# A hybrid decoder layer on one core: the first stage with c as one row, sums of squares as columns, h modulated twice on ScalarE, whole modulation rows, and a block's products by kind

## The chip, the core and the metric

The kernel runs on one core of a Trainium2 chip. The metric is the device time of one execution in microseconds (us). Before the change it is 1109.52 us, the median of three runs (1110.96, 1109.22, 1109.52). Less is better.

## What is computed

One layer of a decoder on 512 tokens of width 1024, everything in float32: a modulated RMSNorm, a mixer of three branches (a state-space scan, dilated window attention, multi-scale pooling), and an MLP with squared ReLU. The change touches only the beginning: the conditioning vector, the first norm, and the first two of the products of h with the columns of w_in, called Q and K.

```python
cond = silu(c)                                    # c is 1 x 1024
sh1, sc1, g1, sh2, sc2, g2 = split(cond @ w_ada + b_ada, 6)
h = rms(x, norm1_w) * (1 + sc1) + sh1             # 512 x 1024
z, xbc, dt_raw, q, k, v, u, gates = split(h @ w_in)
x = x + g1 * mixer(q, k, v, u, gates, z, xbc, dt_raw)
h = rms(x, norm2_w) * (1 + sc2) + sh2
x = x + g2 * (square(relu(h @ w_ff1)) @ w_ff2)
```

## The kernel before

**Layout.** Activations lie with features on partitions: x is held as eight tiles xT[k] of 128 features by 512 tokens. A *block* k, in what follows, is one such step of 128 features. The result h is kept as eight such tiles too, each as a rounded part (hh) and the remainder (hl), and as copies of both with the tokens sorted by residue modulo four (rh, rl). The bulk of the work is steps of 12 products on TensorE (PE): for 128 features and 512 output columns, four accumulators, and for each three products of 512 columns (low x high, high x high, high x low of the split operands; mm3 in the code). Weights are split the same way: ScalarE (ACT) casts the raw weight to a rounded part (wh), and VectorE (DVE) subtracts it for the rest (wl).

**Buffers.** 59 blocks of 128x512 are handed out and taken back by name (blk, free), eight PSUM banks likewise. Later weights come as pairs of blocks, 128x1024, through three pools of three buffers each: raw, wh and wl (wstream, wsplit; lines 272 and 273). One weight pair feeds two steps, 24 products.

**The first stage** (from line 334) is written as one schedule by hand for VectorE, ScalarE, TensorE and SyncE (SP): there each engine does its work in the order of the code. c comes by two transfers of SP, each of 512 values spread over all 128 partitions (crow), and goes through Silu. Then SP brings the eight tiles of x, with vec (per-feature vectors: biases, norm weights) and the identity matrix (cst) in between, and for each block two rows of w_ada as four half rows (wa, 128x512 each, line 231) and two raw weights of Q and K (wst). The sums of squares for the norm: ScalarE squares the eight tiles, VectorE adds them in pairs, and TensorE multiplies them with ones over 512 columns, so that the sums stand on all partitions; four VectorE instructions with the identity (diag, line 416) take them back to columns, ScalarE takes the root, VectorE improves the reciprocal by a Newton step. The four columns are turned into a row again by diagonal matrices and four products with ones (rp). Warm-up products fill TensorE's waits (WARM, line 394).

A block then runs so: four dots of half a w_ada row with crow on VectorE (line 368) and three instructions on one column (lines 374 to 377) give the scale and the shift of the 128 features (A1); ScalarE scales xT (u, line 450), VectorE multiplies with the norm's row R1 (line 451), ScalarE adds the shift and rounds (hh, line 454), VectorE takes the remainder (hl, line 459), ScalarE makes the two copies by residue (line 445). ScalarE and VectorE split the block's two raw weights (lines 383 and 387). TensorE does the block's 24 products, 12 of Q and 12 of K, accumulator by accumulator.

**Behind the first stage** the order of each engine is no longer that of the code: a list scheduler places each instruction at build time where its priority and the buffers it needs allow it. Lines that are marked with high_priority (the weight stream, the copies out of PSUM) are taken earlier. What follows the stage: ScalarE copies q and k out of PSUM (line 324), makes 32 sums of squares of them, one for each 128 columns (sqj, line 511), and TensorE goes on with the next product of 512 columns, whose weights come through the raw, wh and wl pools. I call it Q+1 (accumulators psacc_848 to 851 before, psacc_790 to 793 after). Between two of its weight pairs stand 16 small products for the step sizes of the scan (psdt, lines 737 to 740), which use a small weight wd that ScalarE casts and VectorE subtracts (lines 731, 732).

**Columns of w_ada for later** (parts 2 to 5) are taken in the background, by half rows with crow (ada_later); crow's two blocks are given back at the end of that.

## Time and profile before

| quantity | value |
|---|---|
| median of three runs | 1109.52 us |
| the profiled execution's own time | 1109.32 us |
| its span in the trace | 1107.5 us |
| TensorE busy (PE) / weight loads (PEld) | 99% / 83% of the span |
| VectorE (DVE) / ScalarE (ACT) / GpSimd (POOL) busy | 54% / 46% / 0% |
| TensorE's granted clock | 1.00 |
| moved by DMA | 134.45 MB, mean 121 GB/s |

The profile shows one execution. Engines that are off the end's path may be idle at no cost. A row such as "L368 DVE SCALAR_TENSOR_TENSOR wa<-wa,crow 128x512 ..." is line 368 of the kernel, the engine, the operation, and out <- in by the program's names. In rows of the timeline the first number is the start, the second the time that the row's instructions cover, both in us, and the brackets hold the idle time before them and what ended it. In rows of groups the numbers behind the bar are the total in us and the mean of one in ns. In rows of waits they are the total in us, the number of waits and the longest.

### The profile page before, as it was taken

To read this page: it belongs to the slowest core of one execution; us is meant where nothing else is said; L and a number is where in the kernel's file an instruction comes from. 1 tells how busy PE (TensorE), PEld (TensorE's weight loads), DVE (VectorE), ACT (ScalarE), POOL (GpSimd) and SP (SyncE) were. 2 spreads that over 40 slices of the span, in tenths; PEclk is the share of its full clock that TensorE was granted. 3 is DMA by queue.
4 is the path that set the end of the run, shared out by engine and by line. 5 is a ranking of instruction groups with operands and counts; after the bars stand their busy time and mean duration, and the time that the engine had idled before them with its cause. 6 is when DMAs were issued, how large, how long until landed. Compare 5 with 4: busy or idle time off the path is not lost.

```text
span 1107.5 us, 14079 instructions
## 1 busy us (share of the span) xinstructions
PE 1098.5 (99%) x5414; PEld 916.5 (83%) x5414; DVE 597.1 (54%) x1210; ACT 507.5 (46%) x953; POOL 0.2 (0%) x4
## 2 busy tenths in 40 slices
PE   8999999999999999999999999999999999999998
PEld 6878888888887888888888888899888888888887
DVE  6964773574766778478832433665544223455241
ACT  6895885643596456425422223343433122344120
POOL 0000000000000000000000000000000000000000
PEclk9999999999999999999999999999999999999999
DMA  9943343444543453322323432440133222222241
GB/s 337 314 141 106 115 157 100 133 134 130 186 130 96 125 163 121 119 83 77 123 96 124 143 95 96 142 163 2 60 105 100 96 95 95 96 96 95 95 133 38
DMA packets 49348, 134.45 MB, mean 121 GB/s; under 512 B 5617, under 2 KB 6385, under 8 KB 49281
## 3 DMA queue, kind: packets, MB, share of 16 engines
q1 hardware_dynamic: 47696, 130.81, 36.4%
q10 hardware_dynamic: 1584, 2.75, 0.8%
q8 instruction: 42, 0.69, 0.3%
q14 instruction: 26, 0.20, 0.1%
HBM read 131.41 MB, written 2.13 MB: 121 GB/s over the span
## 4 chain that ended last, share of the span: by engine, by line
PE 89%; ACT 4%; DMA 4%; DVE 2%; issue 1%; SPq 0%; ACTq 0%; DVEq 0%
PE psacc L287 27%; PE psacc L289 27%; PE psacc L288 27%; DMA wa<-in_w_ada_dram 1%; PE psS L566 1%; DMA M<-prow 1%; ACT wh L272 1%; PE psy L880 1%; PE pso L682 1%; PE psyo L888 1%; PE pso L680 1%; DVE conv L798 1%; DMA wst<-in_w_in_dram 0%; PE pskT L550 0%; PE pspT L663 0%
## 5 line engine op out<-in xcount | busy, mean ns | idle before, releaser
L273 DVE TENSOR_TENSOR wl<-raw,wh 128x1024 fp32r<-128x1024 f32 x161 | 196.9, 1223 | 335.5 <-ACT wh L272 333.9
L272 ACT CAST wh<-raw 128x1024 fp32r<-128x1024 f32 x161 | 168.9, 1050 | 365.5 <-PE psacc L288 321.4
L287 PE MATMUL psacc<-hl,wh 128*128 128x512 f32 x416 | 166.4, 400 | 0.6 <-ACT prev L843 0.5
L289 PE MATMUL psacc<-hh,wl 128*128 128x512 f32 x416 | 162.3, 390 | 0.0
L288 PE MATMUL psacc<-hh,wh 128*128 128x512 f32 x416 | 162.1, 390 | 0.0
L287 PEld LDWEIGHTS psacc<-hl,wh 128*128 128x128 f32 x416 | 78.2, 188 | 18.3 <-issue 1.2
L288 PE MATMUL psacc<-ah,wh 128*128 128x512 f32 (+1 forms) x242 | 92.1, 381 | 0.0
L288 PEld LDWEIGHTS psacc<-hh,wh 128*128 128x128 f32 x416 | 78.2, 188 | 16.8 <-issue 1.4
L287 PE MATMUL psacc<-al,wh 128*128 128x512 f32 (+1 forms) x242 | 92.1, 381 | 0.0
L289 PE MATMUL psacc<-ah,wl 128*128 128x512 f32 (+1 forms) x242 | 92.0, 380 | 0.0
L289 PEld LDWEIGHTS psacc<-hh,wl 128*128 128x128 f32 x416 | 78.1, 188 | 16.6
L288 PE MATMUL psacc<-gh,wh 128*128 128x512 f32 x224 | 87.2, 389 | 0.0
L287 PE MATMUL psacc<-gl,wh 128*128 128x512 f32 x224 | 87.2, 389 | 0.0
L289 PE MATMUL psacc<-gh,wl 128*128 128x512 f32 x224 | 87.0, 389 | 0.0
L287 PE MATMUL psacc<-wl,rh 128*128 128x512 f32 x192 | 77.1, 402 | 0.0
L289 PE MATMUL psacc<-wh,rl 128*128 128x512 f32 x192 | 75.2, 392 | 0.0
L288 PE MATMUL psacc<-wh,rh 128*128 128x512 f32 x192 | 74.9, 390 | 0.0
L237 DVE SCALAR_TENSOR_TENSOR wa<-wa,crow 128x512 f32<-128x512 f32 x64 | 43.3, 688 | 19.3 <-DMA wa<-in_w_ada_dram 19.0
L287 PEld LDWEIGHTS psacc<-al,wh 128*128 128x128 f32 x242 | 45.5, 188 | 8.9
L288 PEld LDWEIGHTS psacc<-ah,wh 128*128 128x128 f32 x242 | 45.5, 188 | 8.7
L289 PEld LDWEIGHTS psacc<-ah,wl 128*128 128x128 f32 x242 | 45.5, 188 | 8.7
L287 PEld LDWEIGHTS psacc<-gl,wh 128*128 128x128 f32 x224 | 42.1, 188 | 8.7
(350 smaller groups left out, 1955.8 us busy)
## 6 DMA issues: line engine op xcount, KB each, us to landing
raw<-in_w_in_dram SPq DMA_DIRECT2D x80, 512.0 KB, 3.5
raw<-in_w_ff_dram SPq DMA_DIRECT2D x64, 512.0 KB, 3.5
wa<-in_w_ada_dram SPq DMA_DIRECT2D x96, 256.0 KB, 4.1
wst<-in_w_in_dram SPq DMA_DIRECT2D x16, 256.0 KB, 5.4
M<-prow SPq DMA_DIRECT2D x16, 256.0 KB, 3.3
raw<-in_w_ssd_out_dram SPq DMA_DIRECT2D x8, 512.0 KB, 3.5
raw<-in_w_pool_out_dram SPq DMA_DIRECT2D x8, 512.0 KB, 3.4
raw<-in_w_out_dram SPq DMA_DIRECT2D x8, 512.0 KB, 3.5
```

Of the source, the lines that this page charges most:

```text
L237: V.scalar_tensor_tensor(wa[i], wa[i], 1.0, crow[i], ALU.mult, ALU.mult, accum_out=d[:, i : i + 1])
L272: S.copy(wh, raw)
L273: V.tensor_tensor(wl, raw, wh.bitcast(F32), ALU.subtract)
L287: mm(ps, lhsT=wh, rhs=xl, start=first, stop=False)
L288: mm(ps, lhsT=wh, rhs=xh, start=False, stop=False)
L289: mm(ps, lhsT=wl, rhs=xh, start=False, stop=last)
L566: mm(so[b], lhsT=qT[:, b * P : (b + 1) * P], rhs=kT[:, (b + 1) * P - n : (b + 1) * P], start=True, stop=True)
L680: mm(od, lhsT=vs[kb][:, hs], rhs=pT[b // 2][:, cs : cs + P], start=(b == 0), stop=False, skip_group_check=True)
L682: mm(ov[:, b, :], lhsT=vs[b][:, hs], rhs=pT[0][:, b * P : (b + 1) * P], start=False, stop=(gi == 2 and b == 3), skip_group_check=True)
L798: V.scalar_tensor_tensor(t[:, i:], x[:, : T - i], cw[:, 3 - i, n : n + 1], t[:, i:], ALU.mult, ALU.add)
L880: mm(yp[half * 64 : half * 64 + 64, cs], lhsT=X[c][:, (2 * j + half) * 64 : (2 * j + half + 1) * 64], rhs=Ms[half][:, cs], start=True, sto ...
L888: mm(op[:, cs], lhsT=prev[c][:, j * P : (j + 1) * P], rhs=CT[:, cs], start=True, stop=True)
```

## The change

It rewrites the first stage and leaves the rest of the code as it is.

- **c** is loaded as one row of 1024 on one partition, in two transfers that ScalarE's queue issues, goes through Silu there, and is spread over the partitions by two products with a row of ones into PSUM; VectorE copies it to crow2, which is a small tile of its own and no longer two of the 59 blocks. The filler tile gap shrinks from 464 to 448 columns.
- **vec and the identity** are loaded by GpSimd's queue (POOL) and no longer by SP's.
- **Sums of squares**: VectorE adds the first four tiles' squares, and then three of the other four; TensorE takes the sums as columns, by products of each 128 tokens with one column of ones (square_sums). No diagonal is needed to get columns; ScalarE reads the four sums from PSUM twice, for the root and for the variance. The root's table load comes after the squares. Three of the four diagonals for the row R are made on ScalarE.
- **Modulation rows** come whole, 128x1024 (ada_whole), into buffers of the pools raw, wh and wl in turn, those that the weight stream uses later. A block's two dots are over whole rows (line 379 of the changed kernel), the norm's weight goes into the dot, and one addition of a table pre (line 511) gives scale and shift together.
- **h**: VectorE multiplies xT with R1 (normed, line 475), one instruction on ScalarE scales, shifts and rounds to hh, and a second one makes the same in float32 in place (u, line 478); VectorE subtracts (line 482).
- **Products** of a block by kind: high x high and high x low of Q, the same of K, then low x high of both; in the last block Q's are done before K's.
- **Warm-up** products: 12, 1, 5, 5 and 6 in place of 18, 12 and 6.

What the built programs of the two kernels have on ScalarE behind the first stage, before: rl is the last copy by residue, wh a weight pair's cast, wd the small weight, q and k the copies out of PSUM, sqj the square sums, rkr the root for k.

```order
L445 CAST rh_68_265<-hh_249 128x512
L445 CAST rl_76_273<-hl_257 128x512
L272 CAST wh_854<-raw_852 128x1024
L731 CAST wd_887<-wdt_885 128x8x16
L272 CAST wh_892<-raw_890 128x1024
L324 COPY q_739<-psacc_282 128x512
...
L324 COPY k_793<-psacc_289 128x512
...
L511 ACTIVATE sqj_829,ssk_798<-k_793 128x128
L272 CAST wh_950<-raw_948 128x1024
L188 ACTIVATE rkr_832<-ssk_798,epsc_89 128x16
```

And after the change:

```order
L470 CAST rl_74_269<-hl_253 128x512
L271 CAST wh_796<-raw_794 128x1024
L323 COPY q_681<-psacc_282 128x512
...
L323 COPY k_735<-psacc_289 128x512
...
L546 ACTIVATE sqj_771,ssk_740<-k_735 128x128
L766 CAST wd_829<-wdt_827 128x8x16
L189 ACTIVATE rkr_774<-ssk_740,epsc_88 128x16
L271 CAST wh_834<-raw_832 128x1024
L271 CAST wh_892<-raw_890 128x1024
```

Two weight casts and wd's stood ahead of the copies before; now one cast stands there, and wd's cast and the second pair's follow the last square sum.

TensorE at the same place, before: psacc are Q+1's accumulators with weights wh and wl, psdt the small products.

```order
L289 MATMUL psacc_851<-wh_854,rl_70_267 128x512
L287 MATMUL psacc_848<-wl_893,rh_63_260 128x512
...
L289 MATMUL psacc_851<-wh_892,rl_72_269 128x512
L738 MATMUL psdt_920<-hh_242,wd_887 32x512
L740 MATMUL psdt_920<-hl_250,wd_887 16x512
...
L738 MATMUL psdt_920<-hh_249,wd_887 32x512
L287 MATMUL psacc_848<-wl_951,rh_65_262 128x512
```

And after the change:

```order
L288 MATMUL psacc_793<-wh_796,rl_68_263 128x512
L773 MATMUL psdt_862<-hh_238,wd_829 32x512
L775 MATMUL psdt_862<-hl_246,wd_829 16x512
...
L772 MATMUL psdt_862<-hl_251,wd_829 16x512
L286 MATMUL psacc_790<-wl_835,rh_61_256 128x512
...
L288 MATMUL psacc_793<-wh_834,rl_70_265 128x512
L773 MATMUL psdt_862<-hh_243,wd_829 32x512
...
L773 MATMUL psdt_862<-hh_245,wd_829 32x512
L286 MATMUL psacc_790<-wl_893,rh_63_258 128x512
```

The small products stood behind two weight pairs (48 products) in one run of 16; now eleven of them stand behind the first pair (24 products), and five behind the second pair.

VectorE in one turn of the stage's loop (k = 1, which makes ready block 2), before: wa are half rows of w_ada, A the scale and shift, wsl the low parts of Q's and K's raw weights, hl the remainder of h.

```order
L368 SCALAR_TENSOR_TENSOR wa_349,dot_361<-wa_349,crow_78 128x512
L459 SCALAR_TENSOR_TENSOR hl_251<-u_98_319,A_26_127,hh_243 128x512
L368 SCALAR_TENSOR_TENSOR wa_350,dot_361<-wa_350,crow_79 128x512
L368 SCALAR_TENSOR_TENSOR wa_353,dot_372<-wa_353,crow_78 128x512
L374 SCALAR_TENSOR_TENSOR A_27_128<-dot_361,bsc_33_134 128x1
L375 TENSOR_TENSOR A_27_128<-A_27_128,vec_76 128x1
L368 SCALAR_TENSOR_TENSOR wa_354,dot_372<-wa_354,crow_79 128x512
L387 TENSOR_TENSOR wsl_366<-wst_357,wsh_365 128x512
L377 SCALAR_TENSOR_TENSOR A_27_128<-dot_372,vec_76 128x1
L451 TENSOR_TENSOR u_111_379<-u_111_379,R_60_239 128x512
L387 TENSOR_TENSOR wsl_369<-wst_359,wsh_368 128x512
```

And after the change, with wada the whole rows:

```order
L389 TENSOR_TENSOR wsl_309<-wst_300,wsh_308 128x512
L389 TENSOR_TENSOR wsl_312<-wst_302,wsh_311 128x512
L482 TENSOR_TENSOR hl_247<-u_86_294,hh_239 128x512
L475 TENSOR_TENSOR u_96_345<-xT_6_81,R_58_236 128x512
L379 SCALAR_TENSOR_TENSOR wada_347,dot_355<-wada_347,vec_76,crow_78 128x1024
L379 SCALAR_TENSOR_TENSOR wada_349,dot_355<-wada_349,crow_78 128x1024
L511 TENSOR_TENSOR A_26_124<-dot_355,pre_130 128x2
```

Eleven instructions became seven; the low part of h and the norm's product now stand ahead of the dots.

The diff, cut to its core:

```diff
-WARM = (18, 12, 6)
+WARM = (12, 1, 5, 5, 6)
...
-    small([P, 464], "gap")
-    crow = [blk("crow") for _ in range(2)]
+    small([P, 448], "gap")
+    crow2 = small([P, 2, T], "crow")
+    crow = [crow2[:, i, :] for i in range(2)]
...
-            if not background:
-                free(*crow)
...
+        c1 = [blk("c1") for _ in range(2)]
         for i in range(2):
-            nc.sync.dma_start(crow[i], a["c"][:, i * T : (i + 1) * T].broadcast_to([P, T]))
+            nc.scalar.dma_start(c1[i][:1], a["c"][:, i * T : (i + 1) * T])
+        nc.gpsimd.dma_start(vec, a["vec"])
+        nc.gpsimd.dma_start(cst[:, :P], a["const"][:, :P])
...
+        homes = [(raws, "raw"), (wsp, "wh"), (wsp, "wl")]
+
+        def ada_whole(part, k):
+            pool, tag = homes[0]
+            homes.append(homes.pop(0))
+            w = pool.tile([P, 2, T], F32, tag=tag, name=uid("wada"))
+            src = a["w_ada"][part * 8 + k].rearrange("p (i t) -> p i t", i=2)
+            if k:
+                nc.sync.dma_start(w, src)
+            else:
+                for i in range(2):
+                    nc.sync.dma_start(w[:, i, :], src[:, i, :])
+            return w
+
         for k in range(8):
             nc.sync.dma_start(xT[k], a["x"][k])
-            if k == 0:
-                nc.sync.dma_start(vec, a["vec"])
-            if k == 1:
-                nc.sync.dma_start(cst[:, :P], a["const"][:, :P])
-        wa = [ada_load(1, 0)]
-        wa.append(ada_load(0, 0))
+        wa = [ada_whole(1, 0), ada_whole(0, 0)]
...
-        for i in range(2):
-            S.activation(crow[i], crow[i], AF.Silu)
-        S.activation(junk1, epsc, AF.Sqrt)
...
-            x = wa[i][half]
-            V.scalar_tensor_tensor(x, x, 1.0, crow[half], ALU.mult, ALU.mult, accum_out=dots[k, i][:, half : half + 1])
-            free(x)
-        def dot_end(k, i):
-            d, o = dots[k, i], A1[k][:, i : i + 1]
-            if i == 0:
-                V.scalar_tensor_tensor(o, d[:, 0:1], bsc1[:, k : k + 1], d[:, 1:2], ALU.add, ALU.add)
-                V.tensor_tensor(o, o, vc("norm1_w", k), ALU.mult)
-            else:
-                V.scalar_tensor_tensor(o, d[:, 0:1], vc("b_ada", k), d[:, 1:2], ALU.add, ALU.add)
+        pre = small([P, 8, 2], "pre")
+
+        def dot_half(k, i, half, d):
+            x = wa[i][:, half, :]
+            V.scalar_tensor_tensor(x, x, vc("norm1_w", k) if i == 0 else 1.0, crow[half], ALU.mult, ALU.mult, accum_out=d)
+
+        def dot(k, i, d):
+            V.scalar_tensor_tensor(wa[i], wa[i], vc("norm1_w", k) if i == 0 else 1.0, crow2, ALU.mult, ALU.mult, accum_out=d)
...
+        def square_sums(s, first=False, last=False):
+            for b in range(4):
+                mm(sp[:, b : b + 1], lhsT=s[:, b * P : (b + 1) * P], rhs=ones[:, 0:1], start=first and b == 0, stop=last and b == 3, skip_group_check=True)
...
+        cps = [psm("c") for _ in range(2)]
+        for i in range(2):
+            S.activation(c1[i][:1], c1[i][:1], AF.Silu)
+            mm(cps[i], lhsT=ones[:1], rhs=c1[i][:1], start=True, stop=True)
+        for k in range(8):
+            square(k)
+        S.activation(junk1, epsc, AF.Sqrt)
+        warm(WARM[1])
+        add(0, 1)
+        add(1, 2)
+        add(2, 3)
+        V.tensor_copy(crow[0], cps[0])
+        square_sums(sq[3], first=True)
+        warm(WARM[2])
+        add(4, 5)
+        add(5, 6)
+        square_sums(sq[6])
+        square_sums(sq[7], last=True)
+        V.tensor_copy(crow[1], cps[1])
+        free(sq[3], sq[6], sq[7], *cps, *c1)
+        V.scalar_tensor_tensor(pre[:, :, 0], vc("b_ada", 8, 8), 1.0, vc("norm1_w", 0, 8), ALU.add, ALU.mult)
+        V.tensor_copy(pre[:, :, 1], vc("b_ada", 0, 8))
...
+        S.activation(rt, sp[:, :4], AF.Sqrt, scale=1.0 / D, bias=epsc)
+        S.activation(var, sp[:, :4], AF.Identity, scale=1.0 / D, bias=epsc)
...
-            V.tensor_scalar(dg[b], ident, r[:, b : b + 1], None, ALU.mult)
+            if b == 0:
+                V.tensor_scalar(dg[b], ident, r[:, b : b + 1], None, ALU.mult)
+            else:
+                S.mul(dg[b], ident, r[:, b : b + 1])
...
-        def high(k, R):
-            u = us[k] = blk("u1")
-            if k:
-                S.mul(u, xT[k], A1[k][:, 0:1])
-                V.tensor_tensor(u, u, R, ALU.mult)
-            else:
-                V.scalar_tensor_tensor(u, xT[k], A1[k][:, 0:1], R, ALU.mult, ALU.mult)
-            S.activation(hh[k], u, AF.Identity, bias=A1[k][:, 1:2])
-            return by_residue(0, k)
+        def normed(k, R, ts=slice(0, T)):
+            if k not in us:
+                us[k] = blk("u1")
+            V.tensor_tensor(us[k][:, ts], xT[k][:, ts], R[:, ts], ALU.mult)
+
+        def modulate(k, o, ts=slice(0, T)):
+            S.activation(o[:, ts], us[k][:, ts], AF.Identity, bias=A1[k][:, 1:2], scale=A1[k][:, 0:1])
 
         def low(k):
             u = us.pop(k)
-            i = V.scalar_tensor_tensor(hl[k], u, A1[k][:, 1:2], hh[k].bitcast(F32), ALU.add, ALU.subtract)
+            i = V.tensor_tensor(hl[k], u, hh[k].bitcast(F32), ALU.subtract)
...
+            modulate(k, us[k])
+            w_low(Q, k)
+            w_low(K, k)
+            edgeV = low(k)
             if k < 7:
-                wa = [ada_load(1, k + 1), ada_load(0, k + 1)]
+                normed(k + 1, R1)
+                wa = [ada_whole(1, k + 1), ada_whole(0, k + 1)]
                 w_load(k + 1)
-                dot(k + 1, 0, 0)
-                if k:
-                    low(k)
-                dot(k + 1, 0, 1)
+                d = small([P, 2], "dot", 4)
+                dot(k + 1, 0, d[:, 0:1])
+                dot(k + 1, 1, d[:, 1:2])
+                V.tensor_tensor(A1[k + 1], d, pre[:, k + 1, :], ALU.add)
                 w_high(Q, k + 1)
                 w_high(K, k + 1)
-                by_residue(1, k)
-                dot(k + 1, 1, 0)
-                dot_end(k + 1, 0)
-                dot(k + 1, 1, 1)
-                w_low(Q, k + 1)
-                dot_end(k + 1, 1)
-                high(k + 1, R1)
-                w_low(K, k + 1)
-                if k == 6:
-                    edgeV = low(7)
-                    edgeS = by_residue(1, 7)
+            by_residue(0, k)
+            edgeS = by_residue(1, k)
+            if k < 7:
+                modulate(k + 1, hh[k + 1])
             th, tl = toks(hh[k], False), toks(hl[k], False)
-            for ch, ps in ((Q, qps), (K, kps)):
-                wh, wl = wparts[ch, k]
+            def products(ch, ps, t, w, first=False, last=False):
                 for j in range(4):
-                    mm3(ps[j], th[:, j, :], tl[:, j, :], wh, wl, k == 0, k == 7)
+                    mm(ps[j], lhsT=t[:, j, :], rhs=w, start=first, stop=last)
+
+            two = (Q, qps, *wparts[Q, k]), (K, kps, *wparts[K, k])
+            for ch, ps, wh, wl in two:
+                products(ch, ps, th, wh, first=k == 0)
+                products(ch, ps, th, wl)
+                if k == 7:
+                    products(ch, ps, tl, wh, last=True)
+            for ch, ps, wh, wl in two:
+                if k < 7:
+                    products(ch, ps, tl, wh)
                 free(wh, wl)
     nc.sync.dma_start(cst[:, P:ncut], a["const"][:, P:ncut])
     free(R1)
```

68 lines of the change are left out of this document (28 added, 40 removed).

## The prediction

> **What bounds the kernel now.** I read the page first, then the list of TensorE's waits, then the timeline stage by stage, then the groups of instructions for durations. Line 1 of the page:
> ```profile
> PE 1098.5 (99%) x5414; PEld 916.5 (83%) x5414; DVE 597.1 (54%) x1210; ACT 507.5 (46%) x953; POOL 0.2 (0%) x4
> ```
> TensorE is the bound almost throughout. What it waited for (total, times, longest):
> ```profile
> PE pssx L406 <- DVE sq L405: 2.6, 1, 2.6
> PE psacc L287 <- ACT hh L454: 0.5, 2, 0.4
> PE psacc L287 <- ACT prev L843: 0.5, 1, 0.5
> ```
> Behind the first stage about 1 us of waiting is left in a millisecond. So a change to the first stage moves the end one for one, and so does any wait that it opens later. The stretches (us, then busy time and count of PE, PEld, DVE, ACT, POOL, clock, DMA share, GB/s): the head, the first two blocks, blocks two to eight, two weight pairs of the next product (Q+1), and the dt products:
> ```profile
> 0.00:20.26 20.26, 16.09 (x90) 12.51 (x90) 9.61 (x38) 10.73 (x20) 0.20 (x4) 1.00 0.92 324
> 20.26:27.64 7.38, 6.77 (x27) 4.65 (x27) 7.35 (x20) 6.13 (x9) 0.00 (x0) 1.00 1.04 374
> 65.43:76.31 10.88, 10.88 (x49) 8.93 (x48) 3.76 (x19) 10.88 (x69) 0.00 (x0) 1.00 0.21 69
> 76.31:79.80 3.49, 3.49 (x17) 1.51 (x16) 2.57 (x5) 3.47 (x7) 0.00 (x0) 1.00 0.39 88
> ```
> The third row holds 48 products: 10.88 / 48 = 0.227 us each, so a block's 24 take 5.44. The last row holds 15 of the 16 dt products: 0.233 each. Real products start at 20.26; call the end of the stage E, here 65.43.
>
> **The head: what the change takes away.**
> ```profile
> 0.73 0.86 SPq L336 DMA_DIRECT2D crow<-in_c_dram  x2
> 4.51 0.63 ACT L358 ACTIVATE crow<-crow 128x512 f32<-128x512 f32 x1 [2.29 <-DMA crow<-in_c_dram]
> 10.00:12.00 2.00, 1.99 (x5) 0.58 (x4) 1.32 (x2) 1.95 (x4) 0.00 (x0) 1.00 1.05 386
> 11.58 0.63 ACT L401 ACTIVATE sq<-xT 128x512 f32<-128x512 f32 x1
> 15.57 0.30 ACT L418 ACTIVATE rxr<-rxs,epsc 128x4 f32<-128x4 f32 x1 [3.36 <-DVE diag L416]
> 16.26 0.17 DVE L423 RECIPROCAL rxy<-rxr 128x4 f32<-128x4 f32 x1
> 17.06 0.88 DVE L430 TENSOR_SCALAR diag<-cst,rxy 128x128 f32<-128x128 f32 x4
> 20.26 0.50 PE L287 MATMUL psacc<-wsl,hh 128*128 128x512 f32 x1 [0.37 <-ACT hh L454]
> ```
> The queue is saturated (share 1.05 at 386 GB/s, 0.68 us for 256 KB). Two such transfers of c go: the last square starts, its row of x just landed, at 11.58; less 2 x 0.68 that is 10.2. Bound below: a first landing near 4.5 (an estimate, by vec's 4.4 in a row further down) and seven more rows at 0.68 is 9.3, with vec and cst in the queue 9.6. I take 10.2.
>
> The last square ends at 10.8. Sums as columns: two groups of four blocks, two passes each, still follow the last addition. The price of a short pass is that of the warm-up matmuls, 0.11 ((2.84 - 0.28) / 23):
> ```profile
> 14.40 2.84 PE L394 MATMUL pswarm<-ones 128*128 128x128 f32 x24
> 6.24 1.28 ACT L359 ACT_TABLE_LOAD   x1
> ```
> 16 x 0.11 = 1.8, with its tail 12.8. The square root's table load now stands behind the squares: 10.7 + 1.28 + 0.2 = 12.2, hidden by 0.6; if the sums were ready sooner it would be the next thing late. Root 0.30, then reciprocal and three small instructions (0.8 from 16.26 to 17.06 in the trace), and a semaphore: r at 14.0, against 17.06 before.
>
> From r to the first product the old chain takes 3.2 us. The new one: diagonals and their products 1.05, half a normed block 0.40 (half of L453's 0.74, below), one half-row dot 0.61, two dependent small additions 0.4, half a modulation 0.5, and semaphores, some 0.4: 3.35. First product at 17.35.
>
> Durations for the block loop, from the groups up to 55 us, with a pair of 1024-wide instructions from the timeline:
> ```profile
> L368 DVE SCALAR_TENSOR_TENSOR wa<-wa,crow 128x512 f32<-128x512 f32 x30 | 20.1, 688 | 0.6 <-DMA wa<-in_w_ada_dram 0.6
> L454 ACT ACTIVATE hh<-u,A 128x512 fp32r<-128x512 f32 x7 | 5.1, 724 | 7.8 <-DVE u L451 5.3 <-DVE u L453 2.6
> L453 DVE SCALAR_TENSOR_TENSOR u<-xT,A,psrx 128x512 f32<-128x512 f32 x1 | 0.7, 742 | 0.0
> L383 ACT CAST wsh<-wst 128x512 fp32r<-128x512 f32 x16 | 9.1, 620 | 0.0
> 78.71 2.29 DVE L273 TENSOR_TENSOR wl<-raw,wh 128x1024 fp32r<-128x1024 f32 x2
> ```
> Back to back, a 512-wide VectorE instruction takes 0.61 and a 1024-wide one 1.07 to 1.22; whole-row dots are not in the trace, and I take 1.14. From the first half modulation to that of block two: other half 0.42, K cast 0.52, R1 copy 0.48, second modulation 0.72, low 0.61, normed 0.60, two dots 2.28, addition 0.2, modulation 0.75: 6.6. TensorE's 24 products take 5.44, so it waits 1.1, and block two starts at 23.95. In steady state the same circle without the three opening ACT steps (low, normed, dots, addition, two modulations) is 5.2 against 5.44: TensorE sets the pace, with 0.2 in hand. Grouping products by kind changes their order, not their number: nothing. E = 23.95 + 168 x 0.227 = 62.0 to 62.1, **3.4 us earlier**. Bounds: 1.9 (block circle longer, vec late) to 4.4 (x at 9.6, shorter tails).
>
> Vec now comes by Pool's queue, of which this trace has no transfer; it gates VectorE's first additions. The nearest rows are vec itself (4.4 us to landing) and the slowest small transfer, hv (6.1):
> ```profile
> vec<-in_vec_dram SPq DMA_DIRECT2D x1, 75.0 KB, 4.4
> hv<-in_hvec_dram SPq DMA_DIRECT2D x1, 24.0 KB, 6.1
> ```
> Issued near 0.75, it lands between 5.2 and 6.9; the first addition can start near 6. I take the first, its own row; the other would cost up to 0.8. [...]
>
> **Behind the stage: what the change moves.** ScalarE, VectorE and TensorE around E, before:
> ```profile
> 60.81 1.06 ACT L272 CAST wh<-raw 128x1024 fp32r<-128x1024 f32 x1
> 61.76 0.30 ACT L731 CAST wd<-wdt 128x128 fp32r<-128x128 f32 x1
> 61.96 1.05 ACT L272 CAST wh<-raw 128x1024 fp32r<-128x1024 f32 x1
> 62.91 2.04 ACT L324 COPY q<-psacc 128x512 f32<-128x512 f32 x4
> 66.38 1.10 ACT L324 COPY k<-psacc 128x512 f32<-128x512 f32 x2
> L511 ACT ACTIVATE sqj<-q 128x128 f32<-128x128 f32 x16 | 4.8, 336 | 0.0
> L511 ACT ACTIVATE sqj<-k 128x128 f32<-128x128 f32 x16 | 4.7, 314 | 0.0
> 76.32 1.05 ACT L272 CAST wh<-raw 128x1024 fp32r<-128x1024 f32 x1
> 63.05 0.29 DVE L732 TENSOR_TENSOR wd<-wdt,wd 128x128 fp32r<-128x128 f32 x1
> 81.54 2.50 DVE L519 TENSOR_TENSOR k<-k,rky 128x512 f32<-128x512 f32 x4
> 76.31 0.40 PE L738 MATMUL psdt<-hh,wd 128*32 128x512 f32 x1
> ```
> Before, ScalarE casts two weight pairs and wd ahead of the copies and square sums of q and k. TensorE has 48 products to run meanwhile, and the 16 dt products. After, only one pair's cast stands ahead: wd's cast and the second pair's stand behind all 32 square sums, and on TensorE the dt products stand behind 24 products, not 48. The waiting instruction is a dt product; everything on TensorE is queued behind it.
>
> *First wait.* K's first accumulator closes 0.68 before E (three products), so four k copies (q's four touched 2.04) run from E - 0.5 to E + 1.5. Then 32 square sums, 4.8 + 4.7 in the two groups: E + 11.0. wd's cast 0.30, its subtraction 0.29, semaphores: **E + 11.7**. TensorE has 24 products: free at E + 5.45. It waits 6.2.
>
> *Second wait.* Eleven dt products, 11 x 0.233 = 2.6, end at E + 14.3. The second pair's low part stands behind the k scaling on VectorE: reciprocal and three small ones from E + 11.6 (0.9), four scalings 2.4, subtraction 1.22: E + 16.2. TensorE waits 1.9. Later pairs' subtractions follow 1.14 apart, against 5.44 of products each: covered.
>
> Both waits hang on the same ACT chain, in which the square sums are the measured 4.8 + 4.7; 0.2 off in each of the ten smaller steps makes 8.1 into 7.3 to 8.9.
>
> **Sum.** Against the profiled execution, 1109.32 (span 1107.5, 1.8 around it; the median of the runs, 1109.52, is 0.2 above): -3.4 + 6.2 + 1.9 = +4.7. Farther on, TensorE's order differs by a few rows only; the gain is bounded by the 1 us of waits that is there, a loss by about as much; I take none. 1109.5 + 4.7 = **1114.2 us**.
>
> **Rivals.**
> *The clock falls in the 6 us wait.* At the start the warm-up passes go at half pace for about 3.4 us:
> ```profile
> 2.00:4.00 2.00, 2.00 (x11) 2.00 (x10) 0.00 (x0) 0.21 (x2) 0.00 (x0) 1.00 0.95 231
> 9.55 3.30 PE L406 MATMUL pssx<-sq,ones 128*128 128x512 f32 x6 [2.57 <-DVE sq L405]
> ```
> Eleven records touch 2 us there, 24 take 2.84 us later, while the granted clock reads 1.00 in both. After the wait of 2.57 us, six passes of 512 columns take 3.30: at four short passes of 0.11 each they are worth 2.6 at full pace and 5.3 at half, so no fall shows. A wait of 6.2 is not in the trace. With 3.4 us at half pace the dt products end near E + 16.0, still under the second pair's E + 16.2: nothing lost. If half pace reaches into the products behind, up to 3.4 us of them, it costs 1.7: 1115.9. [...] Chance of over 0.5 us: 0.17.
>
> *The head gains little*, because vec comes later still by Pool's queue, or the block circle takes over 5.44 and TensorE waits in each block (0.15 x 7 = 1). With 0.5 left of the gain: 1117.1. For it: only 0.2 in hand. Chance 0.12.
>
> *The head gains all it can.* With x at 9.6, no wait at block two and 2 us off the tails, 3.4 + 0.6 + 1.1 + 2 = 7: 1109.5 - 7 + 8.1 = 1110.6, no change. Chance 0.06.
>
> *The waits stay covered: faster.* One mechanism: wd's cast ends before TensorE has run its 24 products. It decides at E + 5.45 for wd and E + 8 for the second pair. For before, built order and trace agree row for row, so I see no way; then 1109.5 - 3.4 = 1106.1. Chance 0.03.
>
> **Chances.** The forecast itself has 0.62. A measurement of this kernel tells about 0.2%, 2.2 us, from no change. Slower 0.91, same 0.06, faster 0.03. The range, 1112.4 to 1117.0, takes in the bounds of head (1.9 to 4.4) and waits (7.3 to 8.9) and the clock's price, and leaves out the last two rivals and part of the second.
>
> **What would show it.** In the list of TensorE's waits: psdt on VectorE's wd, about 6; psacc on wl, about 2; hh at block two, about 1. In the timeline: last x square near 10.2, first product near 17.4, first product of Q+1 near 62. Wrong if dt products start within 8 us of E, if the first product comes after 19, or if products right behind the wait go at half pace for longer than the dt products.

## The result and the profile after

The changed kernel takes 1121.22 us (median of five runs, 1120.46 to 1122.51) against 1109.52 before: a ratio of 1.0104, 95% interval 1.0089 to 1.0118. It is slower, as forecast, but by 11.7 us and not by 4.7, and it lies outside the range. Its profiled execution took 1121.44 us with a span of 1119.6, 12.1 more than before.

Line 1 of the page after, and from the 40 slices the row of the granted clock, after and then before:

```profile
PE 1105.1 (99%) x5418; PEld 922.0 (82%) x5418; DVE 596.4 (53%) x1161; ACT 510.6 (46%) x958; POOL 1.4 (0%) x6
PEclk8989999999999999999999999999999999999999
```
```profile
PEclk9999999999999999999999999999999999999999
```

TensorE was as fully busy as before, at 99%, and that hides most of what happened. The clock row shows it: before the change it held 9 in all 40 slices, now the first and the third slice fall under 9. In the list of TensorE's waits the first of the two that were forecast behind the stage stands on top, and the second, in front of the second weight pair, is not there:

```profile
PE psdt L773 <- DVE wd L767: 6.6, 1, 6.6
```

The timeline by stage (us, busy time and count of PE, PEld, DVE, ACT, POOL, clock, DMA share, GB/s): the head, block one, blocks two to eight, one weight pair of Q+1, the wait, eleven small products:

```profile
0.00:21.75 21.75, 20.03 (x95) 18.26 (x95) 9.91 (x30) 11.48 (x23) 1.40 (x6) 0.76 0.94 344
21.75:28.67 6.92, 5.76 (x24) 4.35 (x24) 5.64 (x11) 6.07 (x10) 0.00 (x0) 1.00 1.03 399
28.67:68.16 39.49, 39.16 (x168) 31.19 (x169) 35.04 (x67) 33.91 (x44) 0.00 (x0) 1.00 0.68 229
68.16:73.60 5.44, 5.44 (x25) 4.32 (x23) 3.95 (x19) 5.44 (x29) 0.00 (x0) 1.00 0.42 145
73.60:80.36 6.76, 0.17 (x2) 0.00 (x1) 1.47 (x8) 6.76 (x46) 0.00 (x0) 0.82 0.00 0
80.36:84.95 4.59, 4.59 (x12) 1.67 (x12) 4.45 (x10) 4.16 (x5) 0.00 (x0) 0.52 0.38 114
```

The first product of Q starts at 21.75, where it was 20.26 and was forecast at 17.35. The stage ends at E = 68.16, where it was 65.43 and was forecast at 62.05. To the third weight pair of Q+1, behind all the small products, the two traces read (after, then before):

```profile
91.59 0.39 PE L286 MATMUL psacc<-wl,rh 128*128 128x512 f32 x1
```
```profile
80.02 0.39 PE L287 MATMUL psacc<-wl,rh 128*128 128x512 f32 x1
```

So the 12.1 us came in four parts: 1.5 up to the first product; 1.2 from there to E (46.41 against 45.17); 8.8 from E to the third pair (23.43 against 14.59); and 0.5 in all the rest. The first stage, head and blocks together, from which 3.4 us were to be gained, lost 2.7.

**The head.** TensorE's timeline in the head after the change: warm-up products (pswarm), c's products (psc), the sums of squares (pssx), the row R (psrx), the first product of Q (psacc). Behind it the clock in stretches of 3.41 us, a third of the time that it was 0.50:

```profile
1.09 5.41 PE L396 MATMUL pswarm<-ones 128*128 128x128 f32 x24 [1.09 <-DVE ones L367]
6.43 1.98 PE L419 MATMUL psc<-c,ones 1*128 1x512 f32 x4
8.94 1.19 PE L403 MATMUL pssx<-ones,sq 128*128 128x1 f32 x8
...
12.26 3.41 PE L403 MATMUL pssx<-ones,sq 128*128 128x1 f32 x16
15.54 2.48 PE L396 MATMUL pswarm<-ones 128*128 128x128 f32 x10
17.81 1.91 PE L457 MATMUL psrx<-diag,ones 128*128 128x128 f32 x8
21.75 1.23 PE L521 MATMUL psacc<-wsh,hh 128*128 128x512 f32 x4 [0.52 <-ACT hh L478]
```
```profile
6.29:9.70 3.41, 3.30 (x15) 1.72 (x13) 2.56 (x5) 2.83 (x5) 0.00 (x0) 1.00 1.05 394
9.70:13.11 3.41, 3.41 (x18) 3.41 (x17) 3.16 (x9) 2.44 (x4) 0.00 (x0) 0.50 1.06 398
...
16.53:19.94 3.41, 3.41 (x17) 3.41 (x17) 1.36 (x6) 1.49 (x4) 0.00 (x0) 0.50 1.03 400
19.94:23.35 3.41, 2.89 (x18) 2.33 (x18) 2.63 (x8) 2.25 (x5) 0.00 (x0) 1.00 1.04 400
```

From 9.70 to 19.94 the granted clock was 0.50. A short pass, 0.11 us in my sum, took 0.21 there (3.41 for 16). And the clock fell although the 3.41 us ahead of it, 6.29 to 9.70, read 3.30 busy. What filled most of them were c's products, which use one row of the array, and sums of squares with one column. (The clock's row reads 1.00 ahead of 6.29 too, although the 24 warm-up passes take 0.23 each there; the half pace of the start does not show in it.) This is the theory to be tested: such products occupy TensorE's time, but hardly count as work for the clock.

### The profile page after: what moved, and what is told of

Its sections match the earlier page's. It is cut to its first block, busy times and chain, and to the rows that moved or that the text cites. A ratio compares the mean times of both kernels' runs of the same rounds, so it can differ in the third digit from the quotient of the medians.

```text
span 1119.6 us, 14047 instructions
## 1 busy us (share of the span) xinstructions
PE 1105.1 (99%) x5418; PEld 922.0 (82%) x5418; DVE 596.4 (53%) x1161; ACT 510.6 (46%) x958; POOL 1.4 (0%) x6
## 4 chain that ended last, share of the span: by engine, by line
PE 90%; DVE 4%; ACT 4%; DMA 1%; issue 0%; SPq 0%; ACTq 0%; DVEq 0%
PE psacc L286 27%; PE psacc L288 27%; PE psacc L287 27%; DVE wada L379 1%; ACT sqj L546 1%; PE psS L601 1%; PE psy L915 1%; PE pso L717 1%; ACT u L478 1%; PE psyo L923 1%; ACT hh L478 1%; PE pso L715 1%; DMA M<-prow 1%; PE psst L874 0%; PE pskT L585 0%; DMA xT<-in_x_dram 0%
## 5 line engine op out<-in xcount | busy, mean ns | idle before, releaser
L287 PEld LDWEIGHTS psacc<-hh,wh 128*128 128x128 f32 x416 | 78.2, 188 | 16.9 <-issue 1.4
L287 PEld LDWEIGHTS psacc<-gh,wh 128*128 128x128 f32 x224 | 42.1, 188 | 8.7
```

Of the source, the lines that this page charges most:

```text
L287: mm(ps, lhsT=wh, rhs=xh, start=False, stop=False)
```

## The experiments

Ratios are to runs of the kernel before on the same chip; intervals are 95%. e1 to e4 ran on one chip, e5 to e8 on a second, e9 to e12 on a third, where the kernel before has medians of 1109.82, 1109.20 and 1109.54; a difference in us between rows of two chips is good to about half a microsecond.

| run | edit against the changed kernel | median us | ratio to before | interval |
|---|---|---|---|---|
| changed kernel | none | 1121.22 | 1.0104 | 1.0089 to 1.0118 |
| e1 | 128 rows for c and 128 columns for the sums | 1117.94 | 1.0075 | 1.0060 to 1.0090 |
| e2 | 128 rows for c alone | 1118.49 | 1.0078 | 1.0061 to 1.0094 |
| e3 | 128 columns for the sums alone | 1118.48 | 1.0083 | 1.0068 to 1.0098 |
| e4 | priority for weights and wd behind the stage | 1113.08 | 1.0032 | 1.0020 to 1.0043 |
| e5 | dots ahead of the low part in the loop | 1111.34 | 1.0020 | 1.0011 to 1.0029 |
| e6 | half rows in blocks of their own | 1133.72 | 1.0222 | 1.0207 to 1.0238 |
| e7 | e1 and e5 | 1107.99 | 0.9990 | 0.9981 to 0.9999 |
| e8 | e7, warm-up and one dot earlier | 1107.20 | 0.9983 | 0.9974 to 0.9992 |
| e9 | e6 with gap at 440 columns | 1136.80 | 1.0245 | 1.0231 to 1.0259 |
| e10 | gap at 456 columns, nothing else | 1133.70 | 1.0217 | 1.0203 to 1.0231 |
| e11 | e8, two moves around block 0 | 1105.89 | 0.9969 | 0.9956 to 0.9981 |
| e12 | e8, products by accumulator | 1111.81 | 1.0028 | 1.0016 to 1.0040 |

### The clock in the head: e1, e2, e3

e1 has both edits of the following diff, e2 the first (c), e3 the second (the sums):

```diff
         for i in range(2):
+            V.memset(c1[i], 0.0)
             nc.scalar.dma_start(c1[i][:1], a["c"][:, i * T : (i + 1) * T])
...
-            mm(cps[i], lhsT=ones[:1], rhs=c1[i][:1], start=True, stop=True)
+            mm(cps[i], lhsT=ones, rhs=c1[i], start=True, stop=True)
...
-                mm(sp[:, b : b + 1], lhsT=s[:, b * P : (b + 1) * P], rhs=ones[:, 0:1], ...
+                mm(sp[:, b * P : (b + 1) * P], lhsT=s[:, b * P : (b + 1) * P], rhs=ones, ...
...
-        S.activation(rt, sp[:, :4], AF.Sqrt, scale=1.0 / D, bias=epsc)
+        S.activation(rt, sp[:, ::P], AF.Sqrt, scale=1.0 / D, bias=epsc)
```

Expected of e1:

> The changed kernel with two edits on TensorE alone: c is spread by products over all 128 rows (127 of them zeros, c's tile is cleared first) instead of one row, and the sums of squares are taken with 128 columns of ones instead of one, so that each pass takes as long as before by the trace (0.11 us) but fills the array. Theory A (the granted clock fell to 0.50 from 9.7 to 19.9 us because one-row and one-column products hardly count as work): the clock stays at 1.00 in the head, the last sum of squares is ready near 12.9 instead of 15.7, the first product of Q starts near 17.5 to 18.5 instead of 21.75, and the whole is 3 to 4 us shorter than the changed kernel, 1117 to 1118. Rival B (the passes are late because they stand in TensorE's queue, and the clock only goes along): first product still at 21 or later, 1121. The waits behind the stage stay as they are, 6 to 7 us in front of the small products.

Of e2:

> The changed kernel with c's products over all 128 rows only; the sums of squares stay products with one column. Theory A with the one-row products as the reason: no fall near 9.7; whether one-column products count is then seen in the next window: if they do, as good as with both edits (1117 to 1118); if not, the clock falls about 3.4 us later and 1 to 2 us of the gain are lost (1119 to 1120). Rival B: 1121.

Of e3:

> The changed kernel with sums of squares over 128 columns of ones only; c's products keep one row. Theory A with the one-row products as the reason: the clock falls near 9.7 as before this edit, but, with TensorE filled from there on, it is back at 1.00 near 13 to 16.5 instead of 19.9: first product near 19 to 20, 1119 to 1120. If the one-column products are the reason: no fall, 1117 to 1118. Rival B: 1121.

Measured: e1, the sums, the row and the first product, and its clock in the same stretch:

```profile
11.27 1.95 PE L404 MATMUL pssx<-ones,sq 128*128 128x128 f32 x16
14.77 1.18 PE L458 MATMUL psrx<-diag,ones 128*128 128x128 f32 x8 [0.44 <-DVE diag L455]
17.98 1.23 PE L522 MATMUL psacc<-wsh,hh 128*128 128x512 f32 x4 [0.69 <-ACT hh L479]
```
```profile
12.00:16.00 4.00, 3.56 (x31) 3.37 (x31) 2.75 (x12) 1.91 (x6) 0.00 (x0) 1.00 1.04 402
```

e2 and e3, clock and first product:

```profile
12.00:16.00 4.00, 4.00 (x30) 4.00 (x30) 3.53 (x14) 1.59 (x8) 0.00 (x0) 0.78 1.03 398
19.89 1.22 PE L522 MATMUL psacc<-wsh,hh 128*128 128x512 f32 x4 [0.69 <-ACT hh L479]
```
```profile
8.00:12.00 4.00, 3.63 (x17) 3.44 (x18) 3.90 (x10) 3.81 (x6) 0.00 (x0) 0.59 1.05 396
19.15 1.22 PE L521 MATMUL psacc<-wsh,hh 128*128 128x512 f32 x4 [0.68 <-ACT hh L478]
```

With both edits the clock holds 1.00, sixteen passes take 1.95 instead of 3.41, and the first product comes at 17.98. The passes are as many as in the changed kernel and their operands larger; apart from the warm-up, which starts 1 us later, only what they fill of the array differs. With full rows for c alone (e2), the fall is put off to the one-column sums: the clock is 0.50 from 14.23 to 17.64 (0.61, 0.50, 0.50 and 0.68 in the four slices of 1 us from 14). With full columns alone (e3), it comes at c's one-row products, 0.50 from 8.70 to 12.12 (0.85, three times 0.50, and 0.94 in the five slices of 1 us from 8), and is over sooner. Both medians lie half a microsecond under the 1119 to 1120 that were expected for such a fall, but the traces show it. Both kinds of product leave the clock to fall, each by itself, and theory A stands. Rival B falls: TensorE's queue is as long in e1. The clearing of c's tile delays e1's warm-up by 1 us, which e8 takes back; the clock holds there too (1.00 from 4 to 20). A single run can go the other way: the mean granted clock is 0.997 in three of e1's four runs and 0.995 in the fourth, and 0.995 in three of e2's and 0.997 in the fourth; why was not followed up. Further on the runs are more and plainer: with both edits and no wait behind the stage (e7, e8, e11) it is 1.000 in 26 of 27 runs and 0.999 in one, with neither edit in the head (e5) 0.994 or 0.995 in all ten. The price of the clock in the head is 3.3 us (1121.22 - 1117.94; e5 against e7, on one chip, 3.35).

The times at a clock of 0.50 are, to 0.01 us, once, twice or three times 3.41: 3.41 us in e2, 3.42 in e3, 6.83 in the changed kernel behind its wait (77.96 to 84.79), 10.24 in its head. The 3.41 us ahead of the fall in the head read 97% busy, those ahead of the fall behind the stage (74.55 to 77.96) 0%, so in this run TensorE's busy time alone does not tell that the clock will fall.

### The wait behind the stage: e4, e5, e6

e4 gives priority to the weights of Q+1 and to wd:

```diff
-        S.copy(wd[:, :, :16], wdt)
-        V.tensor_tensor(wd[:, :, 16:], wdt, wd[:, :, :16].bitcast(F32), ALU.subtract)
+        with tc.high_priority(offset=AHEAD):
+            S.copy(wd[:, :, :16], wdt)
+            V.tensor_tensor(wd[:, :, 16:], wdt, wd[:, :, :16].bitcast(F32), ALU.subtract)
...
-        qps = gemm_tok(w_in, 8, Q + 1, rh, rl, 0)
+        qps = gemm_tok(w_in, 8, Q + 1, rh, rl, None)
```

> The changed kernel with the casts and subtractions of the first weight pairs of Q+1 and of the small weight wd given priority at build time, which puts them ahead of the square sums of q and k again (TensorE then has 48 products before the small ones, as before the change); the first stage is as in the changed kernel. Order theory: the wait of 6.6 us in front of the small products and their half pace go, the head stays at 21.75, E at 68.2: 8 to 9 us shorter than the changed kernel, 1112 to 1113. Rival: ScalarE's square sums are late instead and something behind them (k's scaling, the scores) holds TensorE up: less than 5 us gained, 1116 or more.

Measured: 1113.08, 8.1 less than the changed kernel. The first product of Q+1 and the first small product:

```profile
67.89 0.41 PE L286 MATMUL psacc<-wl,rh 128*128 128x512 f32 x1
78.82 0.40 PE L774 MATMUL psdt<-hh,wd 128*32 128x512 f32 x1
```

Between them are 10.9 us, the 48 products, and no wait; E is 0.3 earlier, as is the first product (21.46), so the head is as slow as in the changed kernel. Place and price of the wait were right. Why the order had changed is the question of the next two. e5 moves the loop's steps:

```diff
-            edgeV = low(k)
+            if k == 0:
+                low(k)
             if k < 7:
                 normed(k + 1, R1)
...
                 w_high(K, k + 1)
+            if k:
+                edgeV = low(k)
             by_residue(0, k)
-            edgeS = by_residue(1, k)
             if k < 7:
                 modulate(k + 1, hh[k + 1])
+            edgeS = by_residue(1, k)
```

> The changed kernel with another order inside the block loop: from block one on VectorE does the next block's norm product and dots ahead of the low part of h, and ScalarE rounds the next h ahead of the low part's copy by residue. All the work, the buffers and the head are as in the changed kernel. Theory (the circle over low part, norm product, two dots, two modulations, 5.57 by the trace, sets the pace and lets ScalarE leave the stage late, which is why the built order puts its square sums first): the pace falls to TensorE's 5.44 to 5.46, the wait in front of the small products goes, 9 to 10 us shorter than the changed kernel, 1111 to 1112. Rival (the pace comes from TensorE's weight loads in the grouping by kind): the pace stays at 5.57 and only the wait goes, 1112.5 to 1113.5.

Measured: 1111.34. In the changed kernel one turn of the loop reads so (ScalarE's second modulation u, VectorE's low part hl, norm product u, two dots, addition A, then the next rounded h):

```profile
39.80 0.82 ACT L478 ACTIVATE u<-u,A 128x512 f32<-128x512 f32 x1
40.65 0.69 DVE L482 TENSOR_TENSOR hl<-u,hh 128x512 fp32r<-128x512 f32 x1 [0.52 <-ACT u L478]
41.27 0.68 DVE L475 TENSOR_TENSOR u<-xT,R 128x512 f32<-128x512 f32 x1
41.87 1.28 DVE L379 SCALAR_TENSOR_TENSOR wada<-wada,vec,crow 128x1024 f32<-128x1024 f32 x1
43.07 1.22 DVE L379 SCALAR_TENSOR_TENSOR wada<-wada,crow 128x1024 f32<-128x1024 f32 x1
44.53 0.82 ACT L478 ACTIVATE hh<-u,A 128x512 fp32r<-128x512 f32 x1 [0.82 <-DVE A L511]
45.40 0.76 PEld L521 LDWEIGHTS psacc<-wsh,hh 128*128 128x128 f32 x4 [0.26 <-ACT hh L478]
```

39.80 to 45.38 is a circle of 5.58, and each block's first weight load waits at its end. In e5 a block takes 5.44 (first product of a block, and of the next):

```profile
44.88 1.07 PE L524 MATMUL psacc<-wsh,hh 128*128 128x512 f32 x4
50.32 0.39 PE L524 MATMUL psacc<-wsh,hh 128*128 128x512 f32 x1
```

and ScalarE leaves the stage (the first weight cast behind the last copy of h) at 60.67, 6.0 ahead of E = 66.64. In the changed kernel it was 65.34, 2.8 ahead of 68.16, and before the change 60.81, 4.6 ahead of 65.43 (e5, then the changed kernel):

```profile
60.67 1.05 ACT L271 CAST wh<-raw 128x1024 fp32r<-128x1024 f32 x1
```
```profile
65.34 1.05 ACT L271 CAST wh<-raw 128x1024 fp32r<-128x1024 f32 x1
```

With this room the build places the casts ahead of the copies of q by itself, without e4's priority. Of the 9.9 us, 1.7 are more than e4 gained, on another chip; by E (66.64 against e4's 67.89) it is 1.25: the pace, and a first product at 21.00 in place of e4's 21.46. The rival falls: the grouping by kind is in e5 what it is in the changed kernel, and a block takes 5.44. e6 tests the other reason that the order could have, the rows in the weights' buffers:

```diff
-        wa = [ada_whole(1, 0), ada_whole(0, 0)]
+        wa = [ada_load(1, 0), ada_load(0, 0)]
...
-                dot(k + 1, 0, d[:, 0:1])
-                dot(k + 1, 1, d[:, 1:2])
+                dot_half(k + 1, 0, 0, d[:, 0:1])
+                dot_half(k + 1, 0, 1, e[:, 0:1])
+                dot_half(k + 1, 1, 0, d[:, 1:2])
+                dot_half(k + 1, 1, 1, e[:, 1:2])
```

> The changed kernel with its whole modulation rows undone: half rows in blocks of their own as before the change, four half dots in a block and one addition more, so that the first stage leaves the raw, wh and wl buffers alone. Theory (ScalarE's late end of the stage is the reason for the wait behind it): the wait of 6 to 7 us stays, 1121 to 1123. Rival (the rows in those buffers keep the next weights out): the wait goes, 1112 to 1114.

Measured: 1133.72, which neither expected. The wait itself answers the question: it is still there with those buffers left alone, so they are not its reason.

```profile
PE psdt L778 <- DVE wd L772: 6.5, 1, 6.5
```

How far ahead of E ScalarE leaves the stage goes with the wait in every run: 2.8 to 3.0 us in the seven that have it (the changed kernel, e1, e2, e3, e6, e9, e10), 4.6 or more in those that do not (before, e5, e7, e8, e11, e12), and 2.8 in e4, where the order was forced. That this lead is what the build goes by is argued from these runs and not shown: the order is made at build time, and what times the build reckons with is not on record.

### The 12 us of e6: e9, e10

In e6 the products of h were slower, in every block and far behind the stage. Its four additional small tiles move every later tile in a partition; e9 took 8 columns off the filler, and e10 added 8 columns to the changed kernel's:

```diff
-    small([P, 448], "gap")
+    small([P, 456], "gap")
```

> The half-row run again, with the filler tile gap 8 columns smaller (440), which takes back the 32 bytes for each partition by which its additional small tiles had moved all later tiles. In the first half-row run the products of h took 0.232 us each in place of 0.227, in the stage and long behind it. Theory (the wait behind the stage is from ScalarE's late end and not from the buffers; the slower products come from the moved addresses alone): products at 0.227 to 0.228, the wait of 6 to 7 us still there, 1121 to 1123. Rival (half rows cost this much by themselves): 1133 again.

> The changed kernel with nothing else than the filler tile gap at 456 columns in place of 448: the same instructions in the same order, all tiles behind it 32 bytes later in each partition. If the addresses alone slow the products: products of h at 0.232, 1131 to 1134. If not: 1121.

Measured: 1136.80 for e9, so that this filler was not the one that undoes the move; what half rows cost by themselves stays open. (Its wait of 6.4 is there too.) But e10 is clear: 1133.70, 12.5 us more than the changed kernel with the same instructions in the same order. Groups of products in e10 (total in us, mean ns of one):

```profile
L286 PE MATMUL psacc<-hl,wh 128*128 128x512 f32 x416 | 168.4, 405 | 0.1
L287 PE MATMUL psacc<-ah,wh 128*128 128x512 f32 (+1 forms) x242 | 92.1, 381 | 0.0
L287 PE MATMUL psacc<-gh,wh 128*128 128x512 f32 x224 | 88.6, 396 | 0.0
```

In the changed kernel the means of these three groups are 400, 381 and 389 ns. Products of 512 columns with hl, hh or gh, whose tiles are allocated ahead of the filler, take 5 to 7 ns more each (hl 405 for 400, hh 396 for 390, gh 396 for 389); those with ah and al, which come behind it as the weights do, take no more (381 in both). There are 3 x 416 products with hl and hh and 3 x 224 with gh and gl. The totals of the three groups with hl and hh grow by 7.2 us, that of gh with wh by 1.4; with 1.4 for each of the other two groups with gh and gl, which is an estimate, that makes 11.4 us, against 11.2 between the two profiled executions (1132.59 and 1121.44). That e6's loss has the same cause is likely by its own means (hl 405, gh 395, ah 381) but not shown, since e9 did not undo it. The diff's own change of gap, from 464 to 448, shows no such cost: the page of before has the same three means.

### Both repairs, and what is left: e7, e8, e11, e12

e7 has the edits of e1 and e5, and nothing new:

> Both repairs together: products over 128 rows and 128 columns in the head, and dots ahead of the low part in the loop. If the two are independent: 9.5 us from the loop and the wait and 3.3 us from the clock, 1108 to 1109, somewhat faster than before the change (1109.5). Rival (the earlier head meets a loop that is fed too late by the transfers): 1110 to 1112.

Measured: 1107.99, 13.2 less than the changed kernel, and 3.3 + 9.9 = 13.2: the two add up (by the ratios too, 0.0029 + 0.0084 against 0.0114). E is at 64.01, 1.4 ahead of before, and this is what the first stage gains once clock and pace are mended. e8 clears c's tile, and issues c's transfers, behind ones, and takes block 0's last dot ahead of its norm product (the second edit is shown):

```diff
-        normed(0, rp, ha)
         dot_half(0, 1, 1, d1[:, 1:2])
         V.tensor_tensor(d0, d0, pre[:, 0, :], ALU.add)
         V.tensor_tensor(A1[0], d0, d1, ALU.add)
+        normed(0, rp, ha)
```

> As the run with both repairs, with VectorE's clearing of c's tile behind that of ones, so that the warm-up starts 1 us earlier, and with the last half dot of block 0 ahead of the first norm product, while VectorE waits for the row R. Expected: first product 0.7 us earlier than with both repairs alone, 1107 to 1108.5. If the wait at block two (1.2 us) grows by what the first product gains, no difference to the run with both.

Measured: 1107.20; the first product moved from 18.37 to 17.40. e11 goes after the wait at block two:

```diff
         w_high(Q, 0)
+        w_high(K, 0)
...
         modulate(0, hh[0], hb)
-        w_high(K, 0)
...
-            if k == 0:
-                low(k)
             if k < 7:
                 normed(k + 1, R1)
+            if k == 0:
+                low(k)
+            if k < 7:
```

> The best run so far with two moves around block 0: ScalarE casts K's first weight ahead of the first modulations, while it waits for scale and shift, and VectorE takes block two's norm product ahead of block 0's low part. By the trace of that run VectorE waits 0.74 and 0.50 us there. Expected: the wait of 1.2 us at block two falls under 0.4, the first product stays at 17.4, 1106 to 1106.6. If the first product comes as much later as block two gains: 1107.2 again.

Measured: 1105.89, ratio 0.9969 (0.9956 to 0.9981), faster than both kernels. First product, and the first of Q+1, which is E:

```profile
17.19 1.22 PE L526 MATMUL psacc<-wsh,hh 128*128 128x512 f32 x4
61.70 0.39 PE L286 MATMUL psacc<-wl,rh 128*128 128x512 f32 x1
```

The wait at block two is gone: its first product starts at 22.99, where it was 24.32 in e8, and the list of waits has no row for it. E is 3.7 ahead of before and the median 3.65: one for one. e12 is e8 with the products of a block by accumulator:

```diff
-            for ch, ps, wh, wl in two:
-                products(ch, ps, th, wh, first=k == 0)
-                products(ch, ps, th, wl)
...
+                for j in range(4):
+                    mm3(ps[j], th[:, j, :], tl[:, j, :], wh, wl, k == 0, k == 7)
```

> The run with both repairs and the earlier dot, with the products of a block accumulator by accumulator as before the change, so that hl is asked for with the third product and not with the seventeenth. If the grouping only changes the order, as I had put it: 1107.2. If it hides the low parts: TensorE waits for hl in each of the first blocks, 1 to 4 us more, 1108 to 1111.

Measured: 1111.81, 4.6 more than e8. The wait for hl, and what the products took behind its longest part:

```profile
PE psacc L288 <- DVE hl L483: 2.7, 2, 1.8
```
```profile
20.17 0.79 PE L288 MATMUL psacc<-wsh,hl 128*128 128x512 f32 x1 [1.83 <-DVE hl L483]
21.19 0.63 PE L287 MATMUL psacc<-wsh,hh 128*128 128x512 f32 x1
23.32 0.40 PE L286 MATMUL psacc<-wsl,hh 128*128 128x512 f32 x1
```

The waits take 2.7, and the clock falls again: from 16.47 to 19.88 TensorE is busy for 1.54 of 3.41 us, from 19.88 to 23.30 the granted clock is 0.50 (0.94 from 19 to 20, 0.84 from 20 to 30), and the products there start 0.43 apart, behind it 0.23. Grouping by kind is what lets TensorE start before the low part is there.

## Why the prediction was wrong, point by point

- **The step that failed: "The price of a short pass is that of the warm-up matmuls, 0.11."** The count of passes was right, and the rate was that of a clock at 1.00. The clock was 0.50 from 9.70 to 19.94, and a pass took 0.21. The sums came at 15.7 in place of 12.8, r at 16.9 in place of 14.0, and the way from r to the first product took 4.9 in place of 3.35, with eight passes for R behind ten warm-up ones, all at half pace. I weighed the clock only for the wait behind the stage. e1 to e3 show the cause. In e1 the same chain, at full clock, ends at 17.98, 0.6 behind the forecast. The prediction's own sign of being wrong, a first product after 19, came.
- **The mis-sized term: the block circle, "5.2 against 5.44".** It measured 5.58: each of the two modulations 0.85 to the next step in place of 0.75, the dots 1.20 and 1.26 in place of 1.14. The rival in which TensorE waits in each block had it at 0.15 for each of seven; it was 0.14, and 0.62 once (50.97 to 57.03, where ScalarE issues a transfer of a table at 50.71, ahead of its second modulation, and that starts 0.5 late). e5 shows that the circle sets the pace.
- **Right: that it is slower, and why.** The time lost behind the stage came at the place that was forecast and with about its size, 8.8 for 8.1. The first stage, forecast earlier, came later.
- **Right: transfers and vec.** The last of the eight squares ended at 10.70 against the 10.8 of the sum (six of them are the row below). Vec was used at 5.84, between my 5.2 and 6.9, long before the last square: its issue starts at 1.25 and it took 4.6 to land.

```profile
5.84 0.21 DVE L537 TENSOR_SCALAR qkw<-vec 128x1 f32<-128x1 f32 x1 [4.81 <-DMA vec<-in_vec_dram]
6.74 3.96 ACT L409 ACTIVATE sq<-xT 128x512 f32<-128x512 f32 x6 [1.60 <-DMA xT<-in_x_dram]
```

- **Right: the wait at block two,** 1.1 forecast, 1.16 measured (from the first product to block two 6.6 and 6.92).
- **Right: the first wait,** 6.2 forecast, 6.59 measured, at the dt products and on wd. **The second wait, 1.9, did not show:** the rival of the falling clock came about (0.50 from 77.96 to 84.79, 6.83 us in place of its 3.4), the eleven small products took 4.59 in place of 2.6 and ended near 84.95, when the second pair's low part was just there. The sum of both, 8.1, measured 8.8. The rival's claim that it would cost almost nothing held: full pace would have bought a wait in its place.
- **Left out: why the order had moved.** I took it from the built programs, without a reason. e6 rules out the rows in the weights' buffers; in e5 another order in the loop, with which ScalarE ends its stage earlier, restores the order behind it. That the earlier end is what does it is argued, not shown.
- **"Grouping products by kind changes their order, not their number: nothing"** was wrong as a reason: in e12 undoing it costs 4.6 us.
- **Small:** 0.5 us in all the rest, where I had put none.

Head (4.4) and loop (1.7) together make 6.1 of the 7.4 us that the forecast missed (3.4 forecast earlier, 2.7 measured later), the part behind the stage 0.7, the rest 0.5.

## What to carry to other kernels

Before costing TensorE's passes at a trace's rate, ask what each fills of the array: here products with one row or one column took their time but did not keep the clock up, and the 10.24 us behind them went at 0.50. Where small operands must be used anyway, fill them up to 128: here c's four passes took 1.88 us with 128 rows (e1) and 1.98 with one (changed kernel), the last sixteen of the sums 1.95 with 128 columns (e1) and 1.84 with one (e2), all at a clock of 1.00. When work moves to another engine, look at when that engine leaves the stage, not only at its sum: in every run here whose order was not forced, the order that was built behind the stage went with it.

## What the runs showed of the hardware

- One-row and one-column products each let the granted clock fall to 0.50: with one row it was 0.50 from 8.70 to 12.12 (e3), with one column from 14.23 to 17.64 (e2). With rows of zeros it did not fall: in e1, where 127 of 128 rows of c's tile were zero, it read 1.00 in every slice from 4 to 25.
- A wait can do the same: 3.41 us with TensorE busy for 1.54 were followed by a clock of 0.50 (e12, 19.88 to 23.30), 3.41 us with 0.00 likewise (changed kernel, 77.96 to 84.79), while 3.42 us with 1.78, in the head of the kernel before (7.92 to 11.34), were followed by 1.00.
- The kernel before loses clock in some runs too. Of its 47 runs beside the experiments, the eight with a mean granted clock of 0.998 took 1109.9 to 1111.0 us, the others 1108.5 to 1110.4; as an estimate, 3.41 us at 0.50 would lower the mean over its span of 1107.5 by 0.0015. Where it is lost no trace shows.
- Moving tiles by 32 bytes in each partition made products of 512 columns with one operand ahead of the move 5 to 7 ns slower (hl 400 to 405, gh 389 to 396), and the whole 12.5 us longer (e10, 1133.70 against 1121.22). Which distances are the good ones was not tried.
